# Output products of the first mixer moved between those of the second, three half products a head in the attention steps, and k of later heads as the first head's filling

## The chip, the cores and the metric

The kernel runs on one core of a Trainium2 chip. The core has five engines with instruction streams of their own: TensorE (PE, matrix products into the banks of PSUM, weight loads shown apart as PEld), VectorE (DVE), ScalarE (ACT), GpSimd (POOL) and SyncE (SP, which issues most of the transfers). They meet at semaphores. The metric is the time of one execution on the device in microseconds (us), as the median over runs. "Clock" is the TensorE clock that the throttle granted, as a share of full speed.

## The reference

One decoder block on x of 1024 positions by 1024 features, in float32. The part that matters here is the mixer:

```python
o_a = swa_sink_attention(qa, ka, va, swa_sinks[l])
cq = rmsnorm(q_lat, q_norm_g[l])
qb = (cq @ w_uq[l]).reshape(B, S, MLA_HEADS, MLA_QK_DIM)
...
ckv = rmsnorm(kv_lat, kv_norm_g[l])
kvb = (ckv @ w_ukv[l]).reshape(B, S, MLA_HEADS, MLA_NOPE_DIM + MLA_V_DIM)
...
o_b = mla_attention(q_nope, q_rope, k_nope, k_rope, vb)
y = jax.nn.sigmoid(g_a) * (o_a @ w_o_swa[l]) + jax.nn.sigmoid(g_b) * (o_b @ w_o_mla[l])
x = x + y @ w_out[l]
```

`o_a` comes from a sliding-window attention, `o_b` from a latent attention with 8 heads, swept causally in blocks of 128 queries. Behind it come a gated feed-forward part and a last norm, which the change leaves alone.

## The kernel before

Every float32 product is made of three matmuls on rounded halves: `split` (L161) writes a high part by a cast on ACT (L163) and the low part as a difference on DVE (L166), and `mm3` (L168 to L174) multiplies high by high, low by high and high by low. So a weight costs a load by SP, a cast on ACT and a difference on DVE before its first matmul (`conv_to` does the two), and `load_to` issues its load.

Up to L1039 the order of PE and SP is written by hand. In the part that the change touches, from L1042, the order on each engine is chosen when the program is built, from the order of the calls and priorities; so instructions may stand earlier or later than the Python lines say. Only the casts of ACT are kept in program order in some places (`held`).

This part is the latent attention and both output products. Everything is kept transposed: features on the 128 partitions, positions along the row, in two halves `sh` of 512 positions. Its stages:

- Ahead of the steps: `prod_k`, `prod_q` and `prod_v` (L1112 to L1148) make keys (6 matmuls a half, for a pair `j` of heads), queries (9) and values (6 a block) from the latents; k and q of later pairs go through memory and are loaded per head by `load_k` and `load_q`.
- 64 steps `t`: 8 heads by 8 query blocks, in the block order 2, 3, 6, 7, 0, 1, 4, 5. A step calls `scores` two steps ahead (L1171: matmuls into the PSUM tile scb, row maximum on DVE L1192, exponential on ACT L1193, inverse sum and scaling on POOL L1194, L1195), `pv` of blocks three steps back (L1213: matmuls into ob at L1231 and L1232, a copy on ACT L1237 and an addition on DVE L1243) and `transposes` (L1198: pTb on PE at L1209, then its cast pth on ACT and its difference ptl on DVE). Between them stands filling for PE: in the first head `first` (k and q of the head pair 3), in heads 1 to 7 half products of `mix_a`.
- `mix_a(dc, sh, c0, n)` (L1270) is the first mixer's output product for output chunk `dc` of 128 features and half `sh`: 12 matmuls oA, of which a half product does 6. Its result is copied by ACT to `ar` (L1286); for chunks 0 to 3 it goes out to memory (L1288) and is loaded again later (L1311). It takes the attention output `oaT`, loaded by `load_oa` and split by `split_oa` (L1253), eight splits in all, and the weight pairs oa 0 to 3, each for two chunks.
- `mix_b(dc, i)` (L1400) is the output stage: for each of the eight chunks in the order `DCS`, POOL multiplies the gate by `ar` (L1407), PE makes the second mixer's product oB, 2 x 12 matmuls with the weight pairs ob 0 to 3, DVE multiplies each half by its gate (L1412), then the two are added (half 0 on DVE, half 1 on POOL, L180) and split into yh (ACT) and yl (DVE), the operand of the last product xo with `w_out`.

Before, 14 of the 16 products oA (7 chunks' worth) run as 28 half products at the positions 1, 2, 5 and 6 of heads 1 to 7; the last two run around the last calls of `pv`. PSUM has eight banks: four for oA, transposes and pv results, two double banks for scores until step 62, then four single ones for the last oA and for oB.

Of the kernel before, what the change touches and what calls it, by code (L numbers as in the profile page):

```python
# [12 lines left out]
ALU = mybir.AluOpType  # L13
# [76 lines left out]
def hybrid_block_kernel(  # L90
# [39 lines left out]
    def psum_phase(name, bufs):  # L130
        if psum:
            psum.pop("cm").close()
        psum["cm"] = ExitStack()
        psum["x"] = psum["cm"].enter_context(tc.tile_pool(name=name, bufs=bufs, space=PSUM))
# [977 lines left out]
    def prod_q(j, s, k0=0, n=3):  # L1112
        w = wuq[j]
        if k0 == 0:
            q_ps[0] = (P1 if j > 1 else PX)("q")
        ps = q_ps[0]
        mm3(ps, [((w[:, 0, k], w[:, 1, k]), (cq[k][0][:, half(s)], cq[k][1][:, half(s)])) for k in range(k0, k0 + n)],
            k0 == 0, k0 + n == 3)
        if k0 + n < 3:
            return  # L1120
        t = U("qns", F32R, (P, 2, 512)) if j else None
        outs = [(t[:, 0], t[:, 1], ps)] if j else [
            (qT[u][0:64, 0, half(s)], qT[u][0:64, 1, half(s)], ps[64 * u:64 * u + 64]) for u in range(2)]
        for hi, lo, src in outs:
            nc.scalar.activation(hi, src, AF.Copy, scale=-SC_B)
            nc.vector.scalar_tensor_tensor(lo, src, -SC_B, hi.bitcast(F32), op0=ALU.mult, op1=ALU.subtract)
        if j:
            nc.sync.dma_start(qn_d[j][:, :, half(s)], t.bitcast(F32))

    def prod_k(j, s):  # L1130
        ps = P1("k")
        mm3(ps, [((wk[0][:, k, blk(j)], wk[1][:, k, blk(j)]), (ckv[k][0][:, half(s)], ckv[k][1][:, half(s)]))
                 for k in range(2)])
        if j == 0:
            for u in range(2):
                split(kT[u][0:64, 0, half(s)], kT[u][0:64, 1, half(s)], ps[64 * u:64 * u + 64])
            return
        t = U("kns", F32R, (P, 2, 512))
        split(t[:, 0], t[:, 1], ps)
        nc.sync.dma_start(kn_d[j][:, :, half(s)], t.bitcast(F32))  # L1140

    def prod_v(b):
        ps = P1("v")
        mm3(ps, [((ckv[k][0][:, blk(b)], ckv[k][1][:, blk(b)]), (wv[0][:, k], wv[1][:, k])) for k in range(2)])
        if b % 2 == 0:
            t = V("vM", F32R, (P, 2, NH, P))
            vM.extend([t[:, 0], t[:, 1]])
        split(vM[b][:, :, 0:HD], vM[b][:, :, HD:P], ps.rearrange("p (h d) -> p h d", d=HD))  # L1148

    def load_k(h):  # L1150
        nc.sync.dma_start(kT[h % 3][0:64].bitcast(F32), kn_d[h // 2, 64 * (h % 2):64 * (h % 2) + 64])

    def load_q(h):
        if h >= 2:
            qT[h] = V("qT", F32R, (P, 2, S))
            nc.sync.dma_start(qT[h][0:64].bitcast(F32), qn_d[h // 2, 64 * (h % 2):64 * (h % 2) + 64])
        t = qT[h]
        for i in range(2):
            nc.sync.dma_start(t[64 + 16 * i:80 + 16 * i].bitcast(F32), qr_d[i, 16 * h:16 * h + 16])
# [11 lines left out]
    def scores(t):  # L1171
        h, n = step(t)
        w = (n + 1) * P
        sc = PX("scb", (P, 1024))
        qh, ql = (qT[h][0:QK, i] for i in range(2))
        kh, kl = (kT[h % 3][0:QK, i] for i in range(2))
        cw = 320 if w == 640 else 512
        for c0 in range(0, w, cw):
            c1 = min(c0 + cw, w)
            kc = slice(c0, c1)  # L1180
            o = slice(c0 // cw * 512, c0 // cw * 512 + c1 - c0)
            nc.tensor.matmul(sc[:, o], qh[:, blk(n)], kh[:, kc], start=True, stop=False)
            nc.tensor.matmul(sc[:, o], qh[:, blk(n)], kl[:, kc], start=False, stop=False)
            nc.tensor.matmul(sc[:, o], ql[:, blk(n)], kh[:, kc], start=False, stop=True)  # L1184
        nm = tiny("nmb")
        p = U("p")
        den = tiny("denb")
        s_, m_, p_ = sc[:, 0:w], mask[:, S - w:], p[:, 0:w]
        if cw == 320:
            s_ = sc.rearrange("p (a c) -> p a c", a=2)[:, :, 0:320]  # L1190
            m_, p_ = (v.rearrange("p (a c) -> p a c", a=2) for v in (m_, p_))
        nc.vector.tensor_tensor_reduce(s_, s_, m_, 1.0, -NEG, op0=ALU.add, op1=ALU.min, accum_out=nm)  # L1192
        nc.scalar.activation(p_, s_, AF.Exp, scale=-1.0, bias=nm, accum_out=den)  # L1193
        nc.gpsimd.tensor_tensor(den, den, neg_one[:, 0:1], op=ALU.pow)  # L1194
        nc.gpsimd.tensor_scalar(p[:, 0:w], p[:, 0:w], den, 0.0, op0=ALU.mult, op1=ALU.add)  # L1195
        live[t] = p
# [52 lines left out]
    def load_oa(g, sh):  # L1249
        oa_raw[(g, sh)] = U("oar", F32, (P, 2, 512)), halves_of((P, 2, 512), True)  # L1250
        nc.sync.dma_start(oa_raw[(g, sh)][0], oa_d[2 * g + sh])

    def split_oa(g, sh, c):  # L1253
        raw, (hi, lo) = oa_raw[(g, sh)] if c == 0 else oa_raw.pop((g, sh))
        split(hi[:, c], lo[:, c], raw[:, c])
        oaT[(2 * g + c, sh)] = (hi[:, c], lo[:, c])
# [44 lines left out]

    wo = {}
    NT = NH * NB
    DCS = (4, 0, 5, 1, 6, 2, 3, 7)

    def load_sigs(dc):
        for i in (dc, 8 + dc):
            load_sig(i)
        if dc < 4:
# [9 lines left out]
    prod_v(0)  # L1319
    load_q(0)  # L1320
    load_q(1)
    prod_k(1, 0)
    prod_k(1, 1)
    prod_q(1, 0)
    prod_q(1, 1)
    prod_v(1)
    prod_v(2)
    prod_v(3)
    nc.vector.memset(mask[:, 0:S - P], 0.0)
    nc.vector.tensor_scalar(mask[:, S - P:], band[:, P:], -1.0, None, op0=ALU.mult)  # L1330
    prod_k(2, 0)
    prod_k(2, 1)
    prod_v(4)
    load_k(2)
    prod_q(2, 0)
    psum_phase("psb", 2)
    scores(0)
    prod_q(2, 1)
    prod_v(5)
    scores(1)  # L1340
    prod_v(6)
    prod_v(7)
    first = {0: lambda: prod_k(3, 0), 1: lambda: prod_k(3, 1), 2: lambda: prod_q(3, 0, 0, 2),
             3: lambda: prod_q(3, 0, 2, 1), 5: lambda: prod_q(3, 1, 0, 2), 6: lambda: prod_q(3, 1, 2, 1)}
    fill = {}
    for i in range(16 - 2):
        for c in range(2):
            fill[NB * (i // 2 + 1) + 4 * (i % 2) + 1 + c] = (i // 2, i % 2, 2 * c)
    pvq = []
    for t in range(NT):  # L1350
        h, n = divmod(t, NB)
        if t + 2 < NT:
            scores(t + 2)
        while pvq and pvq[0][0] <= t:
            pv(*pvq.pop(0)[1:])
        if n == 2 and h + 2 < NH:
            load_q(h + 2)
        if n == 6 and h + 3 < NH:
            load_k(h + 3)
        hh, nn = step(t)  # L1360
        if nn % 2 == 1:
            pvq.append((t + 3, hh, nn // 2))
        e = t - (NT - 8)
        if e == 6:
            psum_phase("psc", 4)
        if t in first:
            first[t]()
        if t in fill:
            dc, sh, c0 = fill[t]
            mix_a(dc, sh, c0, 2, P1("oA") if c0 == 0 else None)  # L1370
        transposes(t)
        held[0] = True
        if t in (1, 5):
            for g in range(2):
                load_oa(g, t // 4)
        if t == 3:
            st.load_to(st.index[("oa", 0)])
        if 4 <= t < 12:
            split_oa(t % 4 // 2, t // 4 - 1, t % 2)
        if t == 7:  # L1380
            st.conv_to(st.index[("oa", 0)])
        if n in (0, 4) and h in (2, 4, 6):
            (st.load_to if n == 0 else st.conv_to)(st.index[("oa", h // 2)])
        if e == 4:
            load_sigs(DCS[0])
        if -3 <= e < 3:
            split_ob((e + 3) // 2, (e + 3) % 2)
        if e in (2, 6):
            st.load_to(st.index[("ob", 2 if e == 2 else 0)])
        if e == 6:  # L1390
            st.conv_to(st.index[("ob", 2)])
        held[0] = False
    rest = [(i // 2, i % 2) for i in range(14, 16)]
    mix_a(*rest[0], 0, 4, PX("oA"))
    for _, hp, j in pvq:
        pv(hp, j)
    for r in rest[1:]:
        mix_a(*r, 0, 4, PX("oA"))

    def mix_b(dc, i):  # L1400
        if dc % 2 == 0:
# [24 lines left out]
    st.conv_to(st.index[("ob", 0)])  # L1426
    new_quads("y")
    for i, dc in enumerate(DCS):
        if i in (1, 2):
            st.load_to(st.index[("ob", (3, 1)[i - 1])])  # L1430
        if 3 <= i < 7:
            st.load_to(st.index[("out", 0, i - 3)])
        if i + 2 < 8:
            load_sigs(DCS[i + 2])
        if i + 1 < 8:
            sigmoids(DCS[i + 1])
        mix_b(dc, i)
        if i in (2, 3):
            st.conv_to(st.index[("ob", (3, 1)[i - 2])])
        if i >= 4:  # L1440
            st.conv_to(st.index[("out", 0, i - 4)])
    st.conv_to(st.index[("out", 0, 3)])
# [415 lines left out]
```

## Time and profile before

| | us |
|---|---|
| median of 3 runs | 1353.74 |
| lowest and highest run | 1353.47, 1355.29 |
| profiled execution | 1357.95 |
| its span, first to last instruction | 1356.1 |
| mean granted clock | 0.995 |

The profiled execution is one of its own, 4.21 us longer than the median. In the profile a matmul's length overlaps the next one's; what PE needs for one is the distance of two starts. A row of the timeline ends with the idle time before the instruction and with what ended it. Rows of one name may come from several tiles; wv, wh and wl are parts of weights here (wv is a tile that holds high and low part), sg a gate tile.

### The profile page before, as it was taken

Reading aid. Unit: us, or ns where it says so; the run is one execution under the profiler, and the core shown is the slowest. Engines: PE = TensorE matmul, PEld = TensorE weight load, DVE = VectorE, ACT = ScalarE, POOL = GpSimd, SP = SyncE. Lnnn points to the kernel's source line nnn. Section 1 sums busy time; section 2 is a strip of 40 time slices with the busy share of each in tenths; the row PEclk is TensorE's granted clock in tenths of the full one; section 3 lists DMA queues with packets and bytes.
Section 4 is the critical chain, followed back from the end, with each engine's and each line's share of the span. In section 5 each row is a group of like instructions: output and inputs, shape, how many; then the busy total and the mean of one; then the engine's idle time right before and its main releaser. Section 6 shows DMA issues by size and latency. Waiting matters only on the chain.

```text
span 1356.1 us, 19021 instructions
## 1 busy us (share of the span) xinstructions
PE 1332.1 (98%) x6564; PEld 1118.5 (82%) x6564; DVE 898.1 (66%) x1462; ACT 637.4 (47%) x1293; POOL 574.5 (42%) x621
## 2 busy tenths in 40 slices
PE   9999999999999999998999999999999999999997
PEld 6899878878888988876887888888888888888886
DVE  6868767776767667675458866666655654664862
ACT  7433767665557667753336232322332332644343
POOL 1115545553224554462031565766665551022521
PEclk9999999999999999998999999999999999999999
DMA  9454322335476430771334353644435425996504
GB/s 357 164 182 155 114 100 85 101 129 179 159 225 198 94 86 17 257 276 42 121 158 140 124 180 140 224 179 178 146 142 176 166 86 184 376 384 243 171 10 146
DMA packets 85311, 223.61 MB, mean 165 GB/s; under 512 B 9632, under 2 KB 16288, under 8 KB 84128
## 3 DMA queue, kind: packets, MB, share of 16 engines
q1 hardware_dynamic: 83776, 220.05, 47.0%
q10 hardware_dynamic: 1440, 2.36, 0.5%
q8 instruction: 52, 0.85, 0.3%
q14 instruction: 43, 0.35, 0.1%
HBM read 151.72 MB, written 70.12 MB: 164 GB/s over the span
## 4 chain that ended last, share of the span: by engine, by line
PE 83%; DVE 5%; issue 4%; POOL 4%; ACT 3%; DMA 1%; POOLq 0%; ACTq 0%; DVEq 0%
PE fa L174 7%; PE fa L172 7%; PE fa L173 7%; PE fb L174 6%; PE fb L172 6%; PE fb L173 6%; PE fd L173 5%; PE fd L174 5%; PE fd L172 5%; PE xo L172 2%; PE xo L173 2%; PE xo L174 2%; PE pTb L1209 2%; PE ob L1232 1%; PE ob L1231 1%
## 5 line engine op out<-in xcount | busy, mean ns | idle before, releaser
L166 DVE TENSOR_TENSOR wl<-wr,wl 128x512 fp32r<-128x512 f32 x150 | 150.0, 1024 | 72.0 <-ACT wl L163 71.6
L166 DVE TENSOR_TENSOR lrv<-lr,lrv 128x1024 fp32r<-128x1024 f32 x77 | 105.2, 1397 | 50.2 <-ACT lrv L163 43.3
L163 ACT CAST lrv<-lr 128x1024 fp32r<-128x1024 f32 x77 | 80.1, 1052 | 96.6 <-PE fd L174 57.4
L172 PE MATMUL fd<-lrv 128*128 128x512 f32 x308 | 119.8, 389 | 0.0
L173 PE MATMUL fd<-lrv 128*128 128x512 f32 x308 | 119.8, 389 | 0.0
L174 PE MATMUL fd<-lrv 128*128 128x512 f32 x308 | 119.8, 389 | 0.0
L177 POOL TENSOR_TENSOR wr<-wr,sm 128x512 f32<-128x512 f32 (+1 forms) x38 | 46.4, 1230 | 146.9 <-DVE wl L166 114.6
L163 ACT CAST wl<-wr 128x512 fp32r<-128x512 f32 x150 | 86.8, 622 | 2.0 <-DVE wr L831 1.7
L1194 POOL TENSOR_TENSOR denb<-denb,neg_one 128x1 f32<-128x1 f32 x64 | 39.2, 613 | 97.0 <-ACT p L1193 84.7
L166 DVE TENSOR_TENSOR wl<-sm,wl 128x512 fp32r<-128x512 f32 x60 | 48.6, 836 | 45.9 <-ACT wl L163 45.8
L310 POOL TENSOR_SCALAR ms<-ss 128x1 f32<-128x1 f32 x32 | 8.5, 265 | 147.6 <-ACT xn L1620 69.1
L172 PEld LDWEIGHTS fd<-lrv 128*128 128x128 f32 x308 | 57.8, 188 | 12.1
L173 PEld LDWEIGHTS fd<-lrv 128*128 128x128 f32 x308 | 57.8, 188 | 12.0
L174 PEld LDWEIGHTS fd<-lrv 128*128 128x128 f32 x308 | 57.8, 188 | 11.9
L1193 ACT ACTIVATE p<-scb,nmb 128x384 f32<-128x384 f32 (+3 forms) x64 | 47.8, 747 | 35.7 <-DVE nmb L1192 32.6
L166 DVE TENSOR_TENSOR ptl<-pTb,pth 128x512 fp32r<-128x512 f32 (+2 forms) x96 | 50.3, 552 | 21.3 <-ACT pth L163 20.9
L1192 DVE CUSTOM_DVE_ANT_0 scb<-scb,mask 128x384 f32<-128x384 f32 (+3 forms) x64 | 48.6, 761 | 14.1 <-PE scb L1184 13.1
L1512 ACT ACTIVATE act<-sm 128x512 f32<-128x512 f32 x11 | 7.0, 633 | 104.9 <-DVE sm L180 104.9
L172 PE MATMUL xo<-wv,yh 128*128 128x512 f32 x120 | 49.0, 408 | 3.3 <-ACT yh L163 2.2
L1195 POOL TENSOR_SCALAR p<-p,denb 128x384 f32<-128x384 f32 (+3 forms) x64 | 48.5, 758 | 6.3
L173 PE MATMUL xo<-wv,yh 128*128 128x512 f32 x120 | 48.3, 402 | 1.3 <-DVE wv L166 1.3
L174 PE MATMUL xo<-wv,yl 128*128 128x512 f32 x120 | 48.2, 402 | 0.0
(356 smaller groups left out, 4288.9 us busy)
## 6 DMA issues: line engine op xcount, KB each, us to landing
lr<-la_d SPq DMA_DIRECT2D x77, 256.0 KB, 5.4
wr<-in_w_gate_dram SPq DMA_DIRECT2D x22, 512.0 KB, 4.3
wr<-in_w_up_dram SPq DMA_DIRECT2D x22, 512.0 KB, 5.3
wd<-in_w_down_dram SPq DMA_DIRECT2D x22, 512.0 KB, 7.3
rb_d<-wd SPq DMA_DIRECT2D x22, 512.0 KB, 2.7
la_d<-sd SPq DMA_DIRECT2D x22, 512.0 KB, 5.5
lr<-rb_d SPq DMA_DIRECT2D x44, 256.0 KB, 5.4
lr<-in_w_down_dram SPq DMA_DIRECT2D x33, 256.0 KB, 5.4
```

The source lines that it names most:

```text
L163: i = nc.scalar.copy(hi, src)
L166: (eng or nc.vector).tensor_tensor(lo, src, hi.bitcast(F32), op=ALU.subtract)
L172: nc.tensor.matmul(ps, ah, bh, start=first and i == 0, stop=False, skip_group_check=go_on)
L173: nc.tensor.matmul(ps, ah, bl, start=False, stop=False, skip_group_check=go_on)
L174: nc.tensor.matmul(ps, al, bh, start=False, stop=last and i == n - 1, skip_group_check=go_on)
L177: eng.tensor_tensor(out, a, b, op=ALU.subtract)
L1192: nc.vector.tensor_tensor_reduce(s_, s_, m_, 1.0, -NEG, op0=ALU.add, op1=ALU.min, accum_out=nm)
L1193: nc.scalar.activation(p_, s_, AF.Exp, scale=-1.0, bias=nm, accum_out=den)
L1194: nc.gpsimd.tensor_tensor(den, den, neg_one[:, 0:1], op=ALU.pow)
L1195: nc.gpsimd.tensor_scalar(p[:, 0:w], p[:, 0:w], den, 0.0, op0=ALU.mult, op1=ALU.add)
L1209: nc.tensor.transpose(pp[:, i], p[:, blk(k0 + i)], ident)
L1231: nc.tensor.matmul(po[:, q_off:], vst, hi[:, kb % 4, q_off:], start=kb == 0, stop=False)
```

## The change

The order of the output chunks becomes 4, 5, 0, 6, 1, 2, 3, 7. Ahead of the steps q of all head pairs is made, and k of pairs 0 and 1 only; k of pairs 2 and 3 becomes the filling of steps 0 to 3. The first head's steps 5 and 6 and the positions 1, 2 and 5 of heads 1 to 7, with step 62, take 24 half products (chunks 0 to 5). The splits of `oaT` stand in steps 0 to 7. Each oa weight pair is loaded six steps ahead of its use and converted two ahead; the fourth is first used after the steps. Four products (chunks 6 and 7) are left: two stand around the last calls of `pv`, one behind each of the first two calls of `mix_b`. The ob weight pairs 3 and 1 are loaded and converted one chunk earlier.

```diff
-    DCS = (4, 0, 5, 1, 6, 2, 3, 7)
+    DCS = (4, 5, 0, 6, 1, 2, 3, 7)
...
     prod_v(0)
     load_q(0)
     load_q(1)
+    prod_v(1)
+    prod_q(1, 0)
+    prod_q(1, 1)
+    prod_v(2)
+    prod_q(2, 0)
+    prod_q(2, 1)
+    prod_v(3)
+    load_oa(0, 0)
+    load_oa(1, 0)
...
+    prod_q(3, 0)
+    prod_q(3, 1)
+    psum_phase("psb", 2)
+    prod_v(4)
+    scores(0)
     prod_k(1, 0)
     prod_k(1, 1)
-    prod_q(1, 0)
-    prod_q(1, 1)
-    prod_v(1)
-    prod_v(2)
-    prod_v(3)
...
-    prod_k(2, 0)
-    prod_k(2, 1)
-    prod_v(4)
-    load_k(2)
-    prod_q(2, 0)
-    psum_phase("psb", 2)
-    scores(0)
-    prod_q(2, 1)
+    scores(1)
     prod_v(5)
-    scores(1)
     prod_v(6)
     prod_v(7)
-    first = {0: lambda: prod_k(3, 0), 1: lambda: prod_k(3, 1), 2: lambda: prod_q(3, 0, 0, 2),
-             3: lambda: prod_q(3, 0, 2, 1), 5: lambda: prod_q(3, 1, 0, 2), 6: lambda: prod_q(3, 1, 2, 1)}
+    load_k(2)
+    first = {0: (2, 0), 1: (2, 1), 2: (3, 0), 3: (3, 1)}
     fill = {}
-    for i in range(16 - 2):
-        for c in range(2):
-            fill[NB * (i // 2 + 1) + 4 * (i % 2) + 1 + c] = (i // 2, i % 2, 2 * c)
+    units = [(u // 2, u % 2, c) for u in range(16 - 4) for c in (0, 2)]
+    slots = [5, 6] + [NB * h + n for h in range(1, NH) for n in (1, 2, 5)] + [NT - 2]
+    for t, u in zip(slots, units):
+        fill[t] = u
+    w_at = {t: u[0] // 2 for t, u in fill.items() if u[0] % 2 == 0 and u[1:] == (0, 0)}
...
         if t in first:
-            first[t]()
+            prod_k(*first[t])
...
-        if t in (1, 5):
-            for g in range(2):
-                load_oa(g, t // 4)
-        if t == 3:
-            st.load_to(st.index[("oa", 0)])
-        if 4 <= t < 12:
-            split_oa(t % 4 // 2, t // 4 - 1, t % 2)
-        if t == 7:
-            st.conv_to(st.index[("oa", 0)])
-        if n in (0, 4) and h in (2, 4, 6):
-            (st.load_to if n == 0 else st.conv_to)(st.index[("oa", h // 2)])
+        if t == 0:
+            load_oa(0, 1)
+            load_oa(1, 1)
+        if t < 8:
+            split_oa(t % 4 // 2, t // 4, t % 2)
+        if t + 6 in w_at or t == 0:
+            st.load_to(st.index[("oa", w_at.get(t + 6, 0))])
+        if t + 2 in w_at:
+            st.conv_to(st.index[("oa", w_at[t + 2])])
...
-    rest = [(i // 2, i % 2) for i in range(14, 16)]
-    mix_a(*rest[0], 0, 4, PX("oA"))
+    rest = [(i // 2, i % 2) for i in range(12, 16)]
+    mix_a(*rest.pop(0), 0, 4, PX("oA"))
     for _, hp, j in pvq:
         pv(hp, j)
-    for r in rest[1:]:
-        mix_a(*r, 0, 4, PX("oA"))
+    mix_a(*rest.pop(0), 0, 4, PX("oA"))
...
-        if i in (1, 2):
-            st.load_to(st.index[("ob", (3, 1)[i - 1])])
+        if i in (0, 1):
+            st.load_to(st.index[("ob", (3, 1)[i])])
...
         mix_b(dc, i)
-        if i in (2, 3):
-            st.conv_to(st.index[("ob", (3, 1)[i - 2])])
+        if rest:
+            mix_a(*rest.pop(0), 0, 4, PX("oA"))
+        if i in (1, 2):
+            st.conv_to(st.index[("ob", (3, 1)[i - 1])])
```

More of the change, by code (lines that the diff above doesn't have):

```diff
@@ L1321, in hybrid_block_kernel @@
     load_q(1)
+    prod_v(1)
[7 more added lines that the diff above has]
+    load_oa(1, 0)
+    nc.vector.memset(mask[:, 0:S - P], 0.0)
+    nc.vector.tensor_scalar(mask[:, S - P:], band[:, P:], -1.0, None, op0=ALU.mult)
+    prod_q(3, 0)
[3 more added lines that the diff above has]
+    scores(0)
     prod_k(1, 0)
     prod_k(1, 1)
-    prod_q(1, 0)
-    prod_q(1, 1)
-    prod_v(1)
-    prod_v(2)
-    prod_v(3)
-    nc.vector.memset(mask[:, 0:S - P], 0.0)
-    nc.vector.tensor_scalar(mask[:, S - P:], band[:, P:], -1.0, None, op0=ALU.mult)
-    prod_k(2, 0)
-    prod_k(2, 1)
-    prod_v(4)
-    load_k(2)
-    prod_q(2, 0)
-    psum_phase("psb", 2)
-    scores(0)
-    prod_q(2, 1)
+    scores(1)
     prod_v(5)
-    scores(1)
     prod_v(6)
     prod_v(7)
-    first = {0: lambda: prod_k(3, 0), 1: lambda: prod_k(3, 1), 2: lambda: prod_q(3, 0, 0, 2),
-             3: lambda: prod_q(3, 0, 2, 1), 5: lambda: prod_q(3, 1, 0, 2), 6: lambda: prod_q(3, 1, 2, 1)}
+    load_k(2)
+    first = {0: (2, 0), 1: (2, 1), 2: (3, 0), 3: (3, 1)}
     fill = {}
-    for i in range(16 - 2):
-        for c in range(2):
-            fill[NB * (i // 2 + 1) + 4 * (i % 2) + 1 + c] = (i // 2, i % 2, 2 * c)
+    units = [(u // 2, u % 2, c) for u in range(16 - 4) for c in (0, 2)]
[3 more added lines that the diff above has]
+    w_at = {t: u[0] // 2 for t, u in fill.items() if u[0] % 2 == 0 and u[1:] == (0, 0)}
     pvq = []
```

## The prediction, made before the changed kernel had run

> **What bounds the kernel now.** The page came first, for the share of TensorE (PE) and its granted clock:
>
> ```profile
> span 1356.1 us, 19021 instructions
> PE 1332.1 (98%) x6564; PEld 1118.5 (82%) x6564; DVE 898.1 (66%) x1462; ACT 637.4 (47%) x1293; POOL 574.5 (42%) x621
> PEclk9999999999999999998999999999999999999999
> ```
>
> PE works for 98% of the span, so only 24 us in all are idle; one slice has a reduced clock, number 19 of 40, at about 610 to 644 us. The waits of PE between 340 and 640 us, the part that the change touches (us in total, times, longest), and the busy time of the engines by stage (length, then PE, PEld, DVE, ACT, POOL, clock, DMA share, GB/s):
>
> ```profile
> PE xo L172 <- ACT yh L163: 2.2, 1, 2.2
> PE oB L174 <- DVE wl L166: 2.1, 1, 2.1
> PE xo L173 <- DVE wv L166: 1.3, 1, 1.3
> PE xo L172 <- ACT wv L163: 1.1, 1, 1.1
> ```
>
> ```profile
> 350.00:380.00 30.00, 30.00 (x134) 24.84 (x133) 19.49 (x32) 13.23 (x23) 10.04 (x8) 1.00 0.58 177
> 400.00:430.00 30.00, 27.86 (x173) 23.20 (x172) 25.04 (x50) 22.23 (x53) 15.24 (x22) 1.00 0.69 201
> 451.36:472.00 20.64, 20.64 (x140) 18.71 (x138) 14.55 (x31) 14.21 (x34) 10.73 (x17) 1.00 0.60 129
> 472.00:492.60 20.60, 20.60 (x138) 18.67 (x137) 13.18 (x30) 13.99 (x33) 10.35 (x17) 1.00 0.27 76
> 569.00:595.00 26.00, 26.00 (x116) 21.36 (x114) 17.02 (x21) 14.88 (x19) 15.53 (x11) 1.00 0.76 286
> 618.00:632.00 14.00, 9.43 (x23) 6.62 (x23) 9.08 (x12) 6.80 (x9) 2.77 (x2) 0.63 0.00 1
> ```
>
> Read by stage. The attention steps (a head is some 20.6 us, 451.36 to 472.00) are PE without a gap, so there a matmul taken out is time gained as long as nothing else is late. The exception is the first head and a half (400 to 430): 2.14 us of PE are idle, with DVE 83% busy. In the output stage (568 to 614) PE is full until 595, then loses 2.1 us and a little more, and behind it the first output block (xo) stalls three times and runs at clock 0.63. Its timeline (start, length, engine, line, idle before and releaser):
>
> ```profile
> 567.82 0.39 PE L172 MATMUL oB<-obT,wh 128*128 128x512 f32 x1
> 598.48 0.50 PE L174 MATMUL oB<-obT,wl 128*128 128x512 f32 x1 [2.15 <-DVE wl L166]
> 619.21 0.50 PE L172 MATMUL xo<-wv,yh 128*128 128x512 f32 x1 [1.07 <-ACT wv L163]
> 620.99 0.61 PE L173 MATMUL xo<-wv,yh 128*128 128x512 f32 x1 [1.28 <-DVE wv L166]
> 625.52 0.80 PE L172 MATMUL xo<-wv,yh 128*128 128x512 f32 x1 [2.22 <-ACT yh L163]
> 631.81 0.39 PE L172 MATMUL xo<-wv,yh 128*128 128x512 f32 x1
> ```
>
> The wait that ends last is the one at 625.52, for the last y: 57.7 us after the first oB matmul (625.52 - 567.82). PE had gone on to xo before 619. So the stage is set by a chain of elementwise work, and PE matmuls inside it are free up to a point. The multiplies that begin chunks 1 and 3 of it, and then one chunk:
>
> ```profile
> 570.74 0.69 DVE L1412 TENSOR_TENSOR sg<-oB,sg 128x512 f32<-128x512 f32 x1
> 584.97 0.68 DVE L1412 TENSOR_TENSOR sg<-oB,sg 128x512 f32<-128x512 f32 x1
> 594.94 0.68 DVE L1412 TENSOR_TENSOR sg<-oB,sg 128x512 f32<-128x512 f32 x1
> 596.14 2.28 DVE L166 TENSOR_TENSOR wl<-wr,wh 128x1024 fp32r<-128x1024 f32 x1
> 600.04 0.68 DVE L1412 TENSOR_TENSOR sg<-oB,sg 128x512 f32<-128x512 f32 x1
> 600.75 1.07 DVE L180 TENSOR_TENSOR sg<-sg,sg 128x512 f32<-128x512 f32 x1
> 601.91 0.62 ACT L163 CAST yh<-sg 128x512 fp32r<-128x512 f32 x1 [2.96 <-DVE sg L180]
> 603.17 0.68 DVE L1412 TENSOR_TENSOR sg<-oB,sg 128x512 f32<-128x512 f32 x1
> 604.00 2.13 POOL L180 TENSOR_TENSOR sg<-sg,sg 128x512 f32<-128x512 f32 x1 [2.73 <-DVE sg L1412]
> 607.86 0.68 DVE L1412 TENSOR_TENSOR sg<-oB,sg 128x512 f32<-128x512 f32 x1
> ```
>
> Multiply, add on DVE, cast, multiply, add on POOL, cast, next chunk: 7.82 us from 600.04 to 607.86, against 24 oB matmuls of 26.00/116 = 0.224 us, 5.4 us.
>
> **The change, part by part.** All sums are in the profiled execution's time, 1357.95 us (span 1356.1 and 1.85 around it), 4.21 above the median of 1353.74; I carry the difference over to the median. The matmuls are the same in number.
>
> *1. Two products (24 matmuls) leave the dense part* for places between the oB products, where the chain covers them: 24 x 0.224 = -5.4 us. The half products in the steps go from 28 to 24, the first head's own filling from 30 matmuls to 36 (k of heads 2 and 3, 24, and two half products), the part ahead of the steps gains 6 (q whole, less k); this part (350 to 380) is full on PE with DVE at 65%, so it is longer by its matmuls alone, which the 24 already count.
>
> *2. Heads 1 to 6 lose the half product of their position 6.* What it covered:
>
> ```profile
> 453.82 0.45 PE L172 MATMUL oA<-wv,wv 128*128 128x512 f32 x1
> 455.26 0.71 PE L1209 MATMUL pTb<-ident,p 128*128 128x128 f32 x5
> 458.21 0.69 ACT L1193 ACTIVATE p<-scb,nmb 128x512 f32<-128x512 f32 x1 [0.21 <-DVE nmb L1192]
> 459.06 0.48 PE L1182 MATMUL scb<-kT,qT 96*128 96x512 f32 x1
> 542.18 0.50 PE L1182 MATMUL scb<-kT,qT 96*128 96x512 f32 x1 [0.34 <-ACT p L1193]
> ```
>
> It is 1.44 us long (453.82 to 455.26). At 459.06 the scores enter a bank that the exponential left at 458.90: no slack even now, and in the last head the same place already costs 0.34. With 1.44 us less ahead of it PE comes earlier, but the exponential comes earlier too, since it follows scores that move along. So 0 (all moves along) to 1.44 a head (nothing does). I take 0.4, from the 0.34 of the last head: 6 x 0.4 = +2.4 (0 to 8.6). The last head, which already pays there, loses a half product too: +0.5 (0 to 1.4).
>
> *3. The first head takes all eight splits of the attention output,* spread over heads 0 and 1 before.
>
> ```profile
> L166 DVE TENSOR_TENSOR wv<-oar,wv 128x512 fp32r<-128x512 f32 x7 | 6.2, 884 | 0.0
> wr<-in_w_gate_dram SPq DMA_DIRECT2D x22, 512.0 KB, 4.3
> ```
>
> DVE: 13.18 for a head (472 to 492.6) + 8 x 0.884 + some 3.5 (an estimate: four differences of k, half the columns of that shape's neighbour at 563.87 below, 0.6 each, and one such weight of 1.2) = 23.8 us busy, in which neighbours overlap a little; PE: 20.6 - 4 x 1.44 + 36 x 0.224 = 22.9 us. Both are full. The old loss of 2.14 goes, a new one comes, at a fuller DVE a little larger: I take 2.5, so +0.4 net (-2.1 if none comes, +2 if it doubles). The weight loads are issued six steps ahead on SP's queue, some 15 us; 512 KB land in 4.3 us, so these cost nothing, and would cost at most those 4.3 once.
>
> *4. The end of the steps.* Before, oA matmuls run while the last transposes are cast:
>
> ```profile
> 559.99 0.48 PE L172 MATMUL oA<-wv,wv 128*128 128x512 f32 x1
> 561.37 1.53 ACT L163 CAST pth<-pTb 128x512 fp32r<-128x512 f32 x4
> 562.75 1.09 ACT L163 CAST wh<-wr 128x1024 fp32r<-128x1024 f32 x1
> 563.87 1.23 DVE L166 TENSOR_TENSOR wl<-wr,wh 128x1024 fp32r<-128x1024 f32 x1
> ```
>
> Now the first oA product there needs a weight pair (the fourth of oa) that is converted only at step 62, together with the third of ob, and both casts stand ahead of the last casts of transposes on ACT, their differences ahead of the last ptl on DVE. Queued behind them are the last two attention products, and behind these everything that follows. Two casts are 2 x 1.09 = 2.2, with both differences 4.6. I take +2.7: by the order the differences mostly overlap the casts. (0 if ACT is early, 4.6 at most.)
>
> *5. The chain of the output stage.* Each of the two moved products puts off the next oB by 12 x 0.224 = 2.7 us. The early chunks of the chain last 7.1 us (570.74 to 584.97 are two), 1.7 more than PE's 5.4, so each makes it late by 1.0 or a little more: +2.2. Against it: from 594.94 to 600.04 two multiplies are 5.1 us apart, where 603.17 - 600.04 = 3.1 is usual; between them stands the difference of the ob pair needed next (596.14, 2.28 us), for which PE waits as well. The change loads and converts that pair one chunk earlier: -2.0, and in the last two chunks the multiplies come earlier by the built order, 1.2. In all -1.0, between -3.2 (the lateness is absorbed) and +2.2 (nothing is regained).
>
> *6. The clock.* From 618.14 (619.21 less its idle 1.07) to 620.99 PE had one matmul in 2.85 us, and after it ran at half. What lies behind the last wait counts: from 625.52 to 631.81 are 15 matmuls in 6.29 us, which at 0.224 would take 3.36: 2.9 us lost. By the built order the first xo block of after finds its weights converted; PE runs 21 matmuls and then waits once, for the last y, some 2.9 us. The one wait of 2.15 at 598.48 had no such effect. If the clock holds, -2.9 us; if it drops as before, 0. I take -2.9, a near call.
> The Trainium skill, page "TensorE: Matmul & The Clock Gate", section "What's actually happening", has the clock at half after at least one idle window of about 3.4 us. By that rule one wait of 2.9 us keeps the clock (-2.9, as taken), but the trace dropped it with a matmul inside 2.85 us, so the rule is not sharp here, and a wait only 0.5 us longer would drop it by either.
>
> Sum: -5.4 + 2.4 + 0.5 + 0.4 + 2.7 - 1.0 = -0.4 without the clock, -3.3 with it: 1354.65 for the profiled execution, 1353.74 - 3.3 = **1350.4** for the median.
>
> **Rivals.** *The clock drops again.* All as above with 0 for part 6: 1353.3, no change. For it: idle time of the same size as at 618 to 621. Against it: one wait, in place of two with three more behind.
> *Slower: the chain regains nothing.* Place: the multiplies of the output stage. Price: part 5 is +2.2 instead of -1.0; the last y then comes 3.2 later than forecast, the wait at the 22nd xo matmul is 6 us, and the clock falls for certain. -5.4 + 2.4 + 0.5 + 0.4 + 2.7 + 2.2 = +2.8: 1356.5. It decides from about 2 us of lateness on. For it: DVE and POOL set the pace at 7 to 7.8 us a chunk, and the copies of the moved products (ar) add to ACT in front of the y casts. Against it: the 2.28 us at 596 do leave the path.
> *More is gained.* The casts of part 4 are early enough (0 instead of +2.7) and the clock holds: 1350.4 - 2.7 = 1347.7. For it: ACT is only 68% busy in a head (13.99 of 20.60). Against it: the weight is needed one step after its cast.
>
> **How the numbers follow.** This kernel's timing can tell about 0.2%, 2.7 us, from no change. The forecast gets 0.40 (faster 0.30, same 0.10), the clock's drop 0.24 (same 0.20, 0.02 on each side), the slower rival 0.26 (slower 0.24), the larger gain 0.10. So faster 0.42, same 0.32, slower 0.26. The range, 1347.0 to 1357.2, holds all four centres, and the upper bound of part 2 alone (6.2 over its value, 1356.6); the forecast's own is 1348 to 1352.5.
>
> **What would show it.** Heads 1 to 6 about 19.6 us long (20.64 - 1.44 + 0.4), with waits of the scores for ACT's p of 0.3 to 0.4; waits of about 2.7 us at the last ob products for ptl or wl; no wait of oB for wl; one wait of xo for yh, of 2 to 4 us, and a clock of 1.00 behind it; the last y some 56.7 us after the first oB. Waits above 1 us in each head, a first oB that is not some 0 to 2 us after where the 24 matmuls less would put it, or a clock of 0.5 after the xo wait would make the prediction wrong.

## The result, and the profile after

| | median us | range | runs |
|---|---|---|---|
| before, in the same series | 1355.66 | 1353.13 to 1357.95 | 11 |
| changed kernel | 1358.75 | 1357.03 to 1364.04 | 11 |

The ratio is 1.0026, with a 95% interval of 1.0013 to 1.0038: 0.26% slower, 3.5 us. The forecast was 3.3 us faster. In the waits of PE between 340 and 645 us of the changed kernel (us in total, times, longest) the old waits for weights in the output stage are gone, and a new one stands at the top:

```profile
PE oA L172 <- ACT wv L163: 3.6, 1, 3.6
PE xo L172 <- ACT yh L163: 3.2, 1, 3.2
PE oB L172 <- DVE sg L1412: 1.4, 2, 0.9
PE pTb L1209 <- ACT ar L1286: 1.2, 1, 1.2
PE scb L1182 <- ACT p L1193: 1.2, 4, 0.4
PE ob L1231 <- DVE ptl L166: 0.8, 1, 0.8
```

The prediction has the first of these only in an aside of its part 3 ("at most those 4.3 once"), and took it as nothing. It stands in the first head. The timeline of the changed kernel there, by engine (SP's own queue shows as SPq):

```profile
395.87 0.52 SPq L1140 DMA_DIRECT2D kn_d<-kns  x1
396.44 1.48 SPq L1251 DMA_DIRECT2D oar<-oa_d  x2
398.01 0.45 SPq L238 DMA_DIRECT2D wr<-in_w_o_swa_dram  x1
...
402.54 0.68 ACT L163 CAST wv<-oar 128x512 fp32r<-128x512 f32 x1
407.05 1.04 ACT L163 CAST wv<-wr 128x1024 fp32r<-128x1024 f32 x1 [3.83 <-DMA wr<-in_w_o_swa_dram]
...
404.23 0.28 PE L1184 MATMUL scb<-kT,qT 96*128 96x256 f32 x1
408.14 0.79 PE L172 MATMUL oA<-wv,wv 128*128 128x512 f32 x1 [3.64 <-ACT wv L163]
408.73 0.63 PE L173 MATMUL oA<-wv,wv 128*128 128x512 f32 x1
```

The first oa weight pair is issued at 398.01, behind a store of k and the two loads of attention output, and lands 9.0 us later, at 407.05. ACT has come to its cast at 403.2 and stands there, with the exponentials queued behind it, and PE, whose next matmul needs that weight, stands from 404.50 to 408.14. Then it runs slowly. The engines by stretch (length, PE, PEld, DVE, ACT, POOL, clock, DMA share, GB/s):

```profile
402.00:404.50 2.50, 2.50 (x18) 2.16 (x17) 2.25 (x4) 1.22 (x3) 0.74 (x2) 1.00 1.14 375
404.50:408.10 3.60, 0.00 (x1) 0.00 (x0) 0.00 (x0) 1.04 (x1) 0.00 (x0) 0.89 0.96 266
408.10:411.30 3.20, 3.16 (x9) 2.46 (x10) 2.94 (x5) 1.06 (x4) 0.09 (x1) 0.50 1.06 381
411.30:414.00 2.70, 2.70 (x13) 2.70 (x12) 0.41 (x2) 2.18 (x5) 2.38 (x4) 0.50 1.07 253
414.00:417.00 3.00, 3.00 (x21) 2.69 (x21) 2.60 (x6) 1.68 (x4) 1.88 (x3) 0.98 0.86 186
```

PE, DVE and POOL are at rest for 3.6 us and ACT until 407.05, the transfers are at 96% or more up to 414, and behind the wait the clock is 0.50 for six more us. The second new place is the end of the steps:

```profile
556.23 1.15 PE L1209 MATMUL pTb<-ident,p 128*128 128x128 f32 x9
558.61 0.44 PE L1209 MATMUL pTb<-ident,p 128*128 128x128 f32 x2 [1.23 <-ACT ar L1286]
559.82 0.39 PE L1231 MATMUL ob<-pth,vM 128*128 128x256 f32 x1 [0.77 <-DVE ptl L166]
560.70 0.64 PE L172 MATMUL oA<-wv,wv 128*128 128x512 f32 x1
...
559.56 1.08 ACT L163 CAST wv<-wr 128x1024 fp32r<-128x1024 f32 x1
560.51 1.08 ACT L163 CAST wh<-wr 128x1024 fp32r<-128x1024 f32 x1
561.46 0.40 ACT L163 CAST pth<-pTb 128x256 fp32r<-128x256 f32 x1
```

```profile
560.50:564.00 3.50, 3.47 (x14) 2.91 (x13) 2.82 (x4) 2.32 (x4) 0.02 (x1) 0.56 0.86 286
```

The two weight casts do stand ahead of the last cast of transposes, two waits come before the first oA there, and the clock falls again (0.56 is the mean of this stretch; it is 0.50 from 560.90 on). Third, the output stage of the changed kernel, from its first oB to the last y:

```profile
569.16 0.39 PE L172 MATMUL oB<-obT,wh 128*128 128x512 f32 x1
628.20 0.50 PE L172 MATMUL xo<-wv,yh 128*128 128x512 f32 x1 [3.20 <-ACT yh L163]
638.82 0.39 PE L174 MATMUL xo<-wv,yl 128*128 128x512 f32 x1
...
572.08 0.69 DVE L1412 TENSOR_TENSOR sg<-oB,sg 128x512 f32<-128x512 f32 x1 [0.58 <-PE oB L174]
580.24 0.69 DVE L1412 TENSOR_TENSOR sg<-oB,sg 128x512 f32<-128x512 f32 x1 [0.97 <-PE oB L174]
589.40 0.69 DVE L1412 TENSOR_TENSOR sg<-oB,sg 128x512 f32<-128x512 f32 x1
```

The last y comes 59.04 us after the first oB (57.70 before), since the first two chunks of the chain take 8.16 and 9.16 us; there is the one wait forecast, 3.20 us, and the clock drops 1.0 us behind its end:

```profile
629.17:632.58 3.41, 3.41 (x9) 2.63 (x9) 2.69 (x5) 1.57 (x2) 0.00 (x0) 0.50 0.00 0
```

**Where the time went.** The two profiled executions do not reach this part at the same time, though the program ahead of it is the same (the last section has the reason). All later figures are therefore counted from the first matmul of k, before first, then after:

```profile
350.56 0.39 PE L172 MATMUL k<-ckv,wv 128*128 128x512 f32 x1
637.05 0.39 PE L174 MATMUL xo<-wv,yl 128*128 128x512 f32 x1
```

```profile
347.42 0.39 PE L172 MATMUL k<-ckv,wv 128*128 128x512 f32 x1
433.69 0.42 PE L1182 MATMUL scb<-kT,qT 96*128 96x384 f32 x1
532.22 0.42 PE L1182 MATMUL scb<-kT,qT 96*128 96x384 f32 x1
```

The 60th xo matmul (637.05 and 638.82) is 286.49 and 291.40 us from there: 4.9 us later. Taking at each mark the lateness, less 0.227 us for every matmul (what a matmul of the two products costs where PE is the bound: 24 of them move between nostage_dve and all3_dve_add below, for 53.72 - 48.28 = 5.44 us) that the change has put ahead of it, and adding it for every one that it has taken from there (12 more at the start of head 2's scores, 18 fewer at head 7's, 24 fewer at the first oB):

| stretch | forecast | measured, profile |
|---|---|---|
| matmuls that left | -5.4 | -5.4 |
| to the start of head 2: 433.69 - 347.42 = 86.27, before 80.29 | +0.8: part 3's 0.4, head 1's 0.4 | 5.98 - 2.72 = +3.3 |
| heads 2 to 6: from 86.27 to 532.22 - 347.42 = 184.80; before 103.05 | +2.0, at 0.4 each | 98.53 - 103.05 + 30 x 0.227 = +2.3 |
| head 7 and the end of the steps | +3.2, with 0.5 for head 7 | +4.4 |
| first oB to last y | -1.0 | +1.3 |
| last y to the 60th xo matmul: 10.62, before 11.53 | -2.9 | -0.9 |
| sum | -3.3 | +4.9 |

The timed runs have 3.5 us of this 4.9; the rows are of one execution each, and the waits and the clock differ between executions.

### The profile page after: what moved, and what is told of

It is laid out like the page before. It is cut to its first block, busy times and chain, and to the rows that moved or that the text cites. A ratio compares the mean times of both kernels' runs of the same rounds, so it can differ in the third digit from the quotient of the medians.

```text
span 1357.8 us, 19019 instructions
## 1 busy us (share of the span) xinstructions
PE 1332.3 (98%) x6564; PEld 1119.9 (82%) x6564; DVE 896.7 (66%) x1462; ACT 637.0 (47%) x1293; POOL 577.2 (43%) x621
## 4 chain that ended last, share of the span: by engine, by line
PE 79%; POOL 6%; issue 5%; DVE 5%; ACT 4%; DMA 1%; POOLq 0%; ACTq 0%; DVEq 0%
PE fa L174 7%; PE fa L172 7%; PE fa L173 7%; PE fb L174 6%; PE fb L172 6%; PE fb L173 6%; PE fd L174 5%; PE fd L172 5%; PE fd L173 5%; POOL p L1195 2%; POOL denb L1194 2%; PE xo L172 2%; PE xo L174 2%; PE xo L173 2%; POOL sg L180 1%
## 5 line engine op out<-in xcount | busy, mean ns | idle before, releaser
L172 PE MATMUL xo<-wv,yh 128*128 128x512 f32 x120 | 48.1, 401 | 3.2 <-ACT yh L163 3.2
L163 ACT CAST pth<-pTb 128x512 fp32r<-128x512 f32 (+2 forms) x96 | 43.3, 484 | 9.2 <-PE pTb L1209 8.6
```

Source lines behind the costliest of these rows:

```text
L163: i = nc.scalar.copy(hi, src)
L172: nc.tensor.matmul(ps, ah, bh, start=first and i == 0, stop=False, skip_group_check=go_on)
```

## The experiments

Twelve edited kernels ran. Each time stands as a ratio to the kernel before on the same chip, with its 95% interval; gains on the changed kernel are against its 1.0026. Marks are of the profiled executions, counted from the first k matmul. No edit leaves out or changes any computation.

| kernel | ratio to before | first oB | first oB to last y | 60th xo |
|---|---|---|---|---|
| before | 1 | 217.26 | 57.70 | 286.49 |
| changed | 1.0026 | 221.74 | 59.04 | 291.40 |
| oa0_early | 0.9988 (0.9980 to 0.9997) | 215.39 | 59.03 | 284.83 |
| oa0_swap | 0.9993 (0.9983 to 1.0002) | 215.62 | 59.03 | 284.99 |
| tail_early | 0.9997 (0.9988 to 1.0006) | 217.14 | 56.84 | 284.11 |
| late34 | 1.0018 (1.0006 to 1.0029) | 218.92 | 57.31 | 287.78 |
| none_in_stage | 1.0053 (1.0040 to 1.0065) | 225.46 | 55.52 | 292.37 |
| all3 | 0.9967 (0.9954 to 0.9979) | 212.49 | 58.48 | 281.37 |
| bef_ob_early | 0.9993 (0.9984 to 1.0001) | 217.24 | 56.48 | 284.00 |
| bef_dve_add | 0.9943 (0.9930 to 0.9955) | 217.24 | 52.04 | 277.91 |
| bef_ob_dve | 0.9943 (0.9931 to 0.9956) | 217.28 | 50.55 | 278.19 |
| bef_ob_dve_dcs | 0.9953 (0.9940 to 0.9967) | 217.27 | 51.62 | 277.91 |
| nostage_dve | 0.9922 (0.9909 to 0.9936) | 217.98 | 48.28 | 274.88 |
| all3_dve_add | 0.9917 (0.9904 to 0.9930) | 212.47 | 53.72 | 274.81 |

Where there is no wait for the last y, the figure under "to last y" is the start of the 22nd xo matmul, which needs it.

**The first weight pair, issued earlier (oa0_early).**

```diff
     load_oa(1, 0)
+    st.load_to(st.index[("oa", 0)])
...
-        if t + 6 in w_at or t == 0:
-            st.load_to(st.index[("oa", w_at.get(t + 6, 0))])
+        if t + 6 in w_at:
+            st.load_to(st.index[("oa", w_at[t + 6])])
```

> The changed kernel with the load of the first oa weight pair issued ahead of the steps (behind load_oa(1, 0)) instead of in step 0. Theory: the 3.6 us wait of the first oA for ACT's wv is a load that lands late (9.0 us, issued behind a store of k on SP); with the load earlier the wait and the half clock behind it go, 4 to 5 us less than the changed kernel, about 1 us below before. Rival: ACT and DVE are full in the first head, the cast comes late anyway; PE still idles 2 us or more there and no more than 1.5 us are gained.

The waits of PE in it, 340 to 650 us, and its first head and a half:

```profile
PE xo L172 <- ACT yh L163: 3.2, 1, 3.2
PE pTb L1209 <- ACT ar L1286: 1.4, 2, 1.2
...
PE scb L1182 <- ACT p L1193: 1.1, 4, 0.4
```

```profile
400.00:430.00 30.00, 29.52 (x190) 25.90 (x189) 24.50 (x54) 23.72 (x56) 15.85 (x24) 1.00 0.62 178
```

The wait is gone and 5.1 us with it (0.9988 against 1.0026): the theory holds. PE idles 0.48 us in this window, where it idled 2.14 before, with DVE as busy (24.50 and 25.04). So the forecast's reason for a loss here, a full DVE, is not borne out: with the weight in time the first head loses less than it did before.

**The same load ahead of two others (oa0_swap).**

```diff
         if t == 0:
+            st.load_to(st.index[("oa", 0)])
             load_oa(0, 1)
```

> The changed kernel with the load of the first oa weight pair issued in step 0 ahead of the two loads of attention output (load_oa) instead of behind them: 1.5 us earlier on SP's queue. Theory: lateness in the queue and the time to land (9.0 us) both count; the wait of the first oA shrinks from 3.6 by about the 1.5 us, to 1.5 to 2.5, and the changed kernel gets 1.5 to 3 us faster. Rival: the landing is late because the transfers of that moment share the engines, so an earlier issue lands no earlier; the wait stays at 3 us or more.

Issued 1.6 us earlier (49.02 us behind the first k matmul against 50.59), the load lands in 5.8 us in place of 9.0. The 3.6 us wait goes altogether, with 0.3 left for the weight's difference on DVE, and 4.5 us are gained: more than the 1.5 to 3 of the theory, and against the rival. What is ahead in the queue costs twice, in the issue and in the landing; both loads of attention output had moved 512 KB each ahead of it.

**The fourth weight pair earlier (tail_early).**

```diff
+        if e == -2:
+            st.load_to(st.index[("oa", 3)])
+        if e == 2:
+            st.conv_to(st.index[("oa", 3)])
         if e == 4:
             load_sigs(DCS[0])
```

> The changed kernel with the fourth oa pair loaded at step 54 and converted at step 58 (instead of 58 and 62). Theory: the casts of oa 3 and ob 2 in front of the last casts of transposes cause the waits of 1.2 and 0.8 us at 557 to 560 and the half clock behind them; with one pair out of the way both waits shrink below 0.5 us, the clock stays at 1.0 there and 2 to 3 us are gained on the changed kernel. Rival: the casts only move into the last head, where the scores already wait for exponentials; the wait appears there and less than 1 us is gained.

Its waits of PE:

```profile
PE xo L172 <- ACT yh L163: 3.0, 1, 3.0
PE oA L172 <- ACT wv L163: 2.8, 1, 2.8
PE scb L1182 <- ACT p L1193: 0.8, 3, 0.3
PE ob L1232 <- DVE ptl L166: 0.5, 1, 0.5
...
PE pTb L1209 <- ACT ar L1286: 0.2, 1, 0.2
```

The waits of 1.2 and 0.8 shrink to 0.2 and 0.5; 3.9 us are gained in time. Head 7 and the end of the steps take 33.74 us from the start of head 7 to the first oB, where the changed kernel has 36.94: 3.2 us. In the profile the 60th xo matmul comes 7.3 us earlier: 2.2 of the rest are the shorter way to the last y (56.84), which was not forecast and stays unexplained, 1.4 the first head, whose wait is 2.8 in this execution, and 0.5 lie behind the last y. The timed 3.9 say that not all of this is in every execution.

**The products of the stage two to three chunks later (late34).**

```diff
-        if rest:
+        if i in (3, 4):
             mix_a(*rest.pop(0), 0, 4, PX("oA"))
```

> The changed kernel with the two products inside the output stage put behind chunks 3 and 4 of it instead of 0 and 1. Theory: the chain of multiplies sets this stage, and the products early in it put off its second and third chunk (8.2 and 9.2 us instead of some 7.2); behind chunks 3 and 4 PE is ahead of the chain and hides them: the last y comes some 57 us after the first oB instead of 59.0, 2 us less than the changed kernel. Rival: DVE and POOL alone set the chain, and the products are free at either place: within 0.7 us of the changed kernel.

The last y comes 57.31 us after the first oB, 1.7 less, as the theory has it to 0.3 us. In time 1.1 us, and the two intervals overlap: the place in the stage is seen in the profile and not told apart by the clock.

**All products ahead of the stage (none_in_stage).**

```diff
-    mix_a(*rest.pop(0), 0, 4, PX("oA"))
+    while rest:
+        mix_a(*rest.pop(0), 0, 4, PX("oA"))
 
     def mix_b(dc, i):
```

> The changed kernel with all four remaining products ahead of the output stage. Theory: the first oB comes 5.4 us later, and the last y 57 us after it instead of 59.0, so 3.4 us more than the changed kernel. Rival: the moved products cost the chain nothing, and 5.4 us are lost in full. Second rival: the products cost the chain as much as they take (5.4), and nothing changes.

3.7 us more than the changed kernel, for 3.4 expected. In the profile the way to the last y is 55.52, that is 3.5 us shorter than with the two products inside, and the first oB is later by 3.7 (of 5.4: head 2 starts at 84.63 against 86.27, since the first head's wait was 2.6 this time, and from the start of head 7 to the first oB it is 5.3 longer). So the move does gain, but not its 5.4: by the profile's 3.5 the chain hides about a third of the two products, by the timed 3.7 two thirds, and it pays for the rest.

**The three edits together (all3).** The first oa load, the fourth pair and the chunks 3 and 4, as above.

> The changed kernel with the three edits together: the first oa load ahead of the steps, the fourth oa pair at steps 54 and 58, the two products of the output stage behind its chunks 3 and 4. Theory: three losses in three places that add up, so the gains of 5.1, 3.9 and 1.1 us add to some 10, and the kernel is 6 to 7 us faster than before (ratio 0.995). Rival: the output stage's chain or the clock at its end takes back what comes early; no more than 5 us are gained on the changed kernel (ratio above 0.999).

4.5 us faster than before, 8 us faster than the changed kernel: between theory and rival. The first oB comes 4.8 us earlier than before. That is a net: 5.4 for the matmuls that left and 3.1 gained in heads 0 and 1 (79.88 at the start of head 2, with 12 matmuls more than before's 80.29), against 3.8 lost from head 2 on. The last y then comes 58.48 after it, 0.8 later than before, with a wait of 2.44 and the clock down again. What is won ahead of the stage is won; what is moved into it is partly paid for.

**The old kernel with the ob pairs earlier (bef_ob_early).**

```diff
-        if i in (1, 2):
-            st.load_to(st.index[("ob", (3, 1)[i - 1])])
+        if i in (0, 1):
+            st.load_to(st.index[("ob", (3, 1)[i])])
...
-        if i in (2, 3):
-            st.conv_to(st.index[("ob", (3, 1)[i - 2])])
+        if i in (1, 2):
+            st.conv_to(st.index[("ob", (3, 1)[i - 1])])
```

> The kernel before with the one part of the change that loads and converts the ob pairs 3 and 1 a chunk earlier, in its old order of chunks. Theory of the prediction: the 2.1 us wait of oB at 598 goes and so do 2 us of the chain; the last y comes 55.7 us after the first oB instead of 57.7, 2 us faster than before. Rival: PE and the chain only trade the wait for a longer one at xo, and the time stays within 0.7 us of before.

The wait of oB for wl is gone, but oB now waits twice, 1.3 us in all, for the multiplies of the chain (DVE sg L1412), and the last y is 1.2 earlier, not 2.0; the wait for it grows to 2.8. In time 0.9 us, with an interval that holds none: undecided between the two.

**The addition on DVE (bef_dve_add).** This probes what sets the output stage.

```diff
-            add(ga[:, cs], ga[:, cs], gb[:, cs], (nc.vector, nc.gpsimd)[sh * (i < 7)])
+            add(ga[:, cs], ga[:, cs], gb[:, cs], nc.vector)
```

> The kernel before with the second half's addition in the output stage on DVE in place of POOL (2.13 us there beside a busy DVE, 0.7 to 1.07 on DVE). Theory: the chain sets the stage, so each of seven chunks is some 1.0 to 1.4 us shorter, down to PE's 5.4: the last y comes 48 to 52 us after the first oB instead of 57.7, and the kernel is 4 to 9 us faster. Rival: PE or the weights of the last product set the end; less than 1 us.

7.7 us faster (0.57%), and the y that was waited for is there when PE comes, 52.04 us after the first oB. The chain did set the stage. Between the first oB and the last y one wait is left, 1.8 us of oB for wl. The window around the last y shows full PE and full clock:

```profile
610.00:625.00 15.00, 15.00 (x67) 12.36 (x66) 10.75 (x14) 6.73 (x9) 0.55 (x1) 1.00 0.00 0
```

**The edits and the addition (all3_dve_add).**

> The three edits and the addition on DVE together. Theory: with a shorter chain PE becomes the bound of the output stage, so the two products inside it are no longer hidden there (they cost up to 5.4 us); the gain of the addition is smaller than on the kernel before by up to that: 9 to 12 us faster than before in all. Rival: chain and PE still overlap and the gains add in full, 11 to 16 us.

11.2 us faster than before (0.83%): with nostage_dve the fastest of this study. Its waits of PE in this part:

```profile
PE scb L1182 <- ACT p L1193: 0.7, 3, 0.3
PE ob L1232 <- DVE ptl L166: 0.5, 1, 0.5
PE oA L172 <- DVE ptl L166: 0.3, 1, 0.3
```

The addition gives 6.8 us here (0.9967 to 0.9917), against 7.7 on the kernel before, which the intervals do not tell apart; and 11.2 lies in the theory's range and in the rival's. So these times leave the two undecided; the next kernel decides.

**All products ahead of the stage, with the addition (nostage_dve).** The edits of oa0_early, tail_early, none_in_stage and bef_dve_add.

> The edits to both weight loads and the addition on DVE, but with all four remaining products ahead of the output stage. Theory: with PE as the bound of the stage its place does not matter, the time is within 1 us of the kernel with two products in the stage (ratio to before 0.991 to 0.9925). Rival: the stage still has room beside the chain; 2 to 5 us slower than that.

0.9922 against 0.9917, and the 60th xo matmul at 274.88 against 274.81: the first oB is 5.5 us later and the way from there to the 22nd xo matmul 5.4 shorter. With PE as the bound of the stage it is the same where the two products stand. The move at the centre of the change is worth something only as long as the chain is slower than PE.

**The old arrangement with both (bef_ob_dve).** The edits of bef_ob_early and bef_dve_add.

> The kernel before with the ob pairs a chunk earlier and the addition on DVE: nothing of the change's moves of products. Theory: once the chain does not set the output stage, PE does everywhere, and where a product stands makes no difference; only the 1.8 us wait for wl goes, so some 2 us faster than with the addition alone (ratio to before 0.993 to 0.9925) and within 2 us of the three edits with the addition. Rival: the moves are worth their 5.4 us there too; it stays 4 us or more behind them.

No gain on the addition alone (0.9943 both). The wait for wl is gone and a wait of 2.1 us for the last y has come, with the clock down behind it: a miss. It stays 3.5 us behind all3_dve_add, between the two expectations. Against nostage_dve, which has the same products ahead of the stage, it is 3.3 us later at the 60th xo matmul, and more than that lies behind the first oB (60.91 us from there, against 56.90).

**The order of chunks (bef_ob_dve_dcs).** As bef_ob_dve, with one line more.

```diff
-    DCS = (4, 0, 5, 1, 6, 2, 3, 7)
+    DCS = (4, 5, 0, 6, 1, 2, 3, 7)
```

> The kernel before with the ob pairs a chunk earlier, the addition on DVE and the changed kernel's order of chunks (4, 5, 0, 6, 1, 2, 3, 7). Theory: the 2.1 us wait of xo for the last y and the half clock behind it come from the order of the chunks in the old kernel; with the new order they go, and it is 2 to 3.5 us faster than with the old order (ratio to before 0.992 to 0.993), at most 1 us behind the kernel with all products ahead of the stage. Rival: the wait comes from elsewhere (gates and products that stand late in the stage); it stays at 1.5 us or more and the time within 1 us of the old order (0.994).

The rival holds: a wait of 1.9 us for y stays and one of 1.0 for a weight's difference comes; 0.9953. The order of chunks is not it. What does keep the old arrangement's last y late in the faster stage stays open. The trace says only which engine is full there: in bef_ob_dve DVE is busy 3.91 of the 4 us from 610 to 614 and PE 3.39; in nostage_dve, whose stage starts 0.65 us later, it is 2.71 and 4.00.

## Why the prediction was wrong

**Part 1**, the 24 matmuls that leave the dense part, was right as a count. As time it is shown by nostage_dve against all3_dve_add: with the two products ahead of the stage the first oB comes 5.5 us later.

**Part 2**, the cover lost in the heads, was right in size: 2.3 us in heads 2 to 6, for 0.4 in each of the five. That is in part luck, for its mechanism is shown only for a small share. Of the four waits of the scores for exponentials one each lies in the first, the second and the last head, so heads 2 to 6 have one of 0.23 (at 509.91) and a smaller one of 0.15; all idle time of PE there is 0.47 us. The rest stands in longer distances between starts. In three of these heads the built order puts four transposes in between the scores of block 4, where the old kernel has all transposes ahead of them:

```profile
448.34 0.30 PE L1183 MATMUL scb<-kT,qT 96*128 96x320 f32 x1
448.70 0.66 PE L1209 MATMUL pTb<-ident,p 128*128 128x128 f32 x4
449.11 0.39 PE L1184 MATMUL scb<-kT,qT 96*128 96x320 f32 x1
```

The stretch of eight transposes and six scores takes 2.03 us there, and 1.76 in the old kernel. No run tests this order.

**Part 3 is the step that failed first.** Its words were that the weight loads are issued six steps ahead, some 15 us, and "cost nothing". For the first pair this is not what the diff says: its load stands at step 0 and its cast at step 3. In the trace that was 5.2 us from the issue (398.01) to ACT's readiness (403.2), and the load took 9.0 where I had taken 4.3, a median from a part of the program with other traffic. The trace of before had the price: this very load took 7.39 us there (issued at 405.65). I also priced the miss at 4.3 "at most", without the clock behind it. oa0_early and oa0_swap, each a move of that one load, give 5.1 and 4.5 us (0.9993 against 1.0026). The part's own argument, DVE at its limit, was not borne out by oa0_early. Put right, this part would have been below zero: oa0_early is at 79.84 at head 2's start, 0.45 us before the old kernel with 12 matmuls more.

**Part 4**, the casts at the end of the steps, was right but for the clock: +2.7 forecast, with 0.5 for the last head 3.2; 4.4 measured. late34 has the same two waits, 1.23 and 0.77, without the clock falling, and takes 35.41 us from the start of head 7 to the first oB in place of 36.94: the clock is 1.5 of the 4.4, and 2.9 is left for the forecast's 3.2. The waits came sooner than forecast, one at the transposes (for ACT's copy ar) and one at the ob products. tail_early takes 3.2 us away.

**Part 5**, the chain of the output stage, had the right bound (bef_dve_add) and the wrong sign. The lateness at the third chunk was to be 2.2 and is 3.1 (589.40 - 569.16 = 20.24, where the old kernel has 584.97 - 567.82 = 17.15). Regained was 1.8, not 3.2: loading the ob pair earlier gives 1.2 of the 2.0 that I read off the interval of the multiplies. none_in_stage measures the whole: the two products cost the chain 3.5 in the profile, and 1.7 by the timed runs (5.4 - 3.7).

**Part 6**, the clock, had the right price: from the last y to the 60th xo matmul it is 11.53 us before and 8.63 in bef_dve_add without a wait, 2.9 us. But the clock did not hold; measured is -0.9 in place of -2.9, as the half clock behind the last y lasted 3.4 us in this execution of after and 5.9 in that of before. The step that failed is the reading of the one wait of 2.15 us without effect as a sign that a single wait of 2.9 is safe. That wait was spared by its place, as the last section works out. In the traces here the clock drops once PE is idle for 1.75 us of a 3.41 us window; a wait of 2.9 escapes only if a border of two windows lies in the right half microsecond of it, about one time in seven (an estimate from these numbers, 0.5 of 3.41). So this was not a near call. Single waits of 2.11 to 3.21 us for y brought the clock down in all eight traces that have one.

The slower rival named the lateness of the chain, which is there (+1.3 of its +2.2), with too high a price and as the sole cause; the largest single loss, in the first head, was in no rival.

## What to carry to other kernels

Follow the first use of a moved stream on its own: a rule like "six steps ahead" has a first element for which it does not hold, and its load queues behind everything that starts there. Take the landing time from the same load in the old trace if it is there, and price a stall of some 1.7 us or more with the slow clock behind it. Work moved under a chain of small operations is only as free as the chain is late at that very place; shortening the chain (here one addition on another engine, 0.57%) was worth more than filling its gaps.

## What the runs showed of the hardware

The clock fell at waits shorter than expected, and the length of a wait alone does not tell whether it falls. In each of the fourteen traces every stretch between two changes of the granted clock lasts a whole number of windows of 3.413 us (the shortest is one, the longest 1334.61 us, 391 of them). Cut into such windows from the first change on, the traces have 24 windows at full clock in which PE is idle for 1.75 us or more, by the profile's modelled ends of matmuls, and the clock is 0.50 in the window behind each of them; it is so behind none of the 5440 windows with 1.61 us or less. The half clock ends behind a window with at most 0.48 us idle and goes on behind those with 0.80 or more. The wait of 2.15 us of before (596.33 to 598.48) was split by a border: 1.40 us idle in one window, with an earlier wait of 0.4, and 1.15 in the next:

```profile
593.91:597.32 3.41, 2.01 (x8) 1.03 (x6) 3.41 (x4) 2.53 (x3) 1.56 (x2) 1.00 0.82 278
597.33:600.74 3.41, 2.26 (x10) 1.89 (x11) 3.39 (x3) 1.58 (x2) 3.41 (x3) 1.00 1.00 338
```

The wait of 1.82 us of bef_dve_add at the same place lies in one window, and the clock is 0.50 from 595.49 to 598.90:

```profile
592.08:595.49 3.41, 1.59 (x8) 1.07 (x7) 3.41 (x2) 0.98 (x2) 3.21 (x2) 1.00 1.03 395
```

The windows lie elsewhere in each execution (the first change is at 4.00 to 10.24 us), so one kernel with one wait can keep the clock in one execution and lose it in the next.

The Trainium skill, page "TensorE: Matmul & The Clock Gate", section "What's actually happening", gives at least one idle window of about 3.4 us for the half clock; these traces agree with the window's length, but here it is enough that PE is idle for about half of it.

The start of the program varies. The first sixteen matmuls into kvq, the same in both programs, took 9.21 us in the profile of before and 7.10 in that of after:

```profile
5.99 9.21 PE L521 MATMUL kvq<-wr,h 128*128 128x512 f32 x16 [1.17 <-DMA wr<-in_w_x_dram]
```

```profile
5.61 7.10 PE L521 MATMUL kvq<-wr,h 128*128 128x512 f32 x16 [0.87 <-DMA wr<-in_w_x_dram]
```

The clock explains this: it is on record only from its first change, to 1.00, at 10.24 us in before and at 4.53 in after. The starts of these matmuls in before are about 0.85 us apart up to 10.24 and 0.43 behind it, in after about 0.43 throughout. The profile shows 1.00 for the time that is not on record.

The first k matmul comes at 347.3 to 350.9 us over the profiles of this study, whichever kernel it is. That is as wide as the effects here, so single executions were compared from that mark on, and kernels by their medians.

The load of the first oa pair, 512 KB, landed in 7.9 to 9.0 us in the four traces in which two others of that size stand just ahead of it at step 0 (after, tail_early, late34, none_in_stage), and in 5.7 to 6.2 in the five in which it was issued ahead of the steps or ahead of these two.
